# The sums among the MLP's weight factors, made in the mixers' last stage and kept in DRAM

## The chip, the cores and the metric

The kernel runs on one core of a Trainium2 chip. The metric is the time of one execution on the device in microseconds (us); the median of three runs is given, and one further execution was profiled.

## The reference, cut to what matters

```python
h = concatenate([meta, x])                       # 16 + 2048 rows of 1024, one layer
z, xbc, dt, u, gates = split(rmsnorm(h) @ w_in)
y_a = ssd_branch(z, xbc, dt, ...)                # gated SSD mixer
y_b = s5_branch(u, ...)                          # S5 mixer, ends in y @ w_glu
g_a, g_b = split(sigmoid(gates))
h = h + (g_a * y_a + g_b * y_b) @ w_out
hn = rmsnorm(h)
h = h + square(relu(hn @ w_ff_in)) @ w_ff_out    # 1024 -> 4096 -> 1024
out = rmsnorm(h)[16:]                            # float32
```

The change touches only how the factors of `w_ff_in` and `w_ff_out` are prepared.

## The kernel before

Every float32 matrix is split into a rounded high part (type float32r, by a copy on ScalarE) and a low part (a subtraction on VectorE or GpSimd), and each product is three matmuls: high by high, high by low, low by high (`mm3`, lines 244 to 246).

**Mixers.** The 2048 rows go through in four blocks `b` of 512. A block has the input products (weights `wu` by `xnh`, `xnl`) with the SSD and S5 work between them, then its last products: GLU (`y5h`, `y5l` by 8 weight units) and OUT (`mixh`, `mixl` by 8 units). Four PSUM banks of the pool `psd` hold a group's four results; `evac_glu` (VectorE on `gth`) and `evac_out` (VectorE adds `xr`, which SP's queue has loaded, and SP stores the sum to `h2d`) empty them before the next group can fill them. In block 0 a unit is loaded raw (`wst`), split, used and stored (`wsd`), all on SP's queue; in later blocks GpSimd's queue loads the finished `wsd`. Three unit buffers stand for this (`NWU`).

**MLP.** It runs over three batches of rows: 768, 768 and 512 (`FB`). Each batch makes 8 passes (`di`) over the hidden width, and each pass 28 products by Strassen-Winograd's scheme: 7 for each half of `w_ff_in`'s block (`ff_in`) and 7 for each half of `w_ff_out`'s (`ff_out`). Such a group of 7 needs 7 weight factors from four quarters of a pair of weight units: three are quarters themselves, and four are sums or differences (s1 to s4, t1 to t4). Only batch 0 makes the factors (`Weights.make`): SP loads a group's two units into two of four `raw` buffers, GpSimd makes the four sums in five `sum` buffers, and `weight` splits each factor into one of three `wc` buffers (ScalarE the high part, line 1344; VectorE or GpSimd the low part, line 1345, by the list `ENG`: 15 and 13 of 28), uses it and stores it to `wcd` (line 1346). Batches 1 and 2 load the finished factors from `wcd` by GpSimd's queue (`read`, line 1355). Factors are traced one product ahead (`AHEAD`).

A pass of batches 0 to 2 begins with ScalarE's first copy `u<-pd` at line 1457 (two copies in a pass, one for each half). Each engine and each queue executes in the order that the program's scheduler wrote; an instruction that waits holds back what stands behind it.

The part of `weight` that the ring of three buffers hangs on:

```python
t = wcs[0].tile([P, 2, n, 512 // n], F32R, name="wc", tag="wc", bufs=wcs[1])   # 3 buffers
S.copy(t[:, 0], w)
(V if eng == "v" else G).tensor_tensor(t[:, 1], w, t[:, 0].bitcast(F32), op=ALU.subtract)
nc.sync.dma_start(wcd[i], t.rearrange("p a k n -> p (a k n)").bitcast(F32))
```

Of the kernel before, what the change touches and what calls it, by code (L numbers as in the profile page):

```python
# [9 lines left out]
F32 = mybir.dt.float32  # L10
F32R = mybir.dt.float32r
AF = mybir.ActivationFunctionType
ALU = mybir.AluOpType
# [3 lines left out]
P = 128  # L17
# [19 lines left out]
NWC = 5  # L37
NWU = 3
NJK = 1
AHEAD = 1  # L40
NRAW = 4
FPACE = 2
# [85 lines left out]
def _body(ctx, tc, d, out):  # L128
# [3 lines left out]
    def pool(name, bufs=1, stack=ctx, **kw):  # L132
        if "space" not in kw:
            kw["reuse_waits"] = "tile"
        return stack.enter_context(tc.tile_pool(name=name, bufs=bufs, **kw))
# [56 lines left out]
    tabd = dr.tile([P, NQ, 2, KA + 1], F32, name="tabd")  # L192
    h2d = dr.tile([SEQ, D], F32, name="h2d")
    xtd = dr.tile([7, P, 4, FB[1][1] // 2], F32, name="xtd")
    wcd = dr.tile([8 * 28, P, D], F32, name="wcd")
    csd = dr.tile([NB, NC4 * NH, P], F32, name="csd")
    ud = dr.tile([NM + SEQ, 512], F32, name="ud")
# [692 lines left out]
        return t  # L890


    xp = pool("xn", stack=xp_st)

    def load_x(pl, r0, L, src):
# [101 lines left out]
    def ff_raw(pl, nm):  # L997
        return pl.tile([P, D], F32, name=nm, tag="raw", bufs=NRAW)
# [90 lines left out]
    for b in range(NB):  # L1089
# [166 lines left out]
            xn = make_xn(gp, b + 1, xp)  # L1256
        mh = gp.tile([P, 8, TB], F32R, name="mixh")
        ml = gp.tile([P, 8, TB], F32R, name="mixl")
        for q in range(4):
            n = q // 2  # L1260

            def evac_glu(c, p):
                th = gp.tile([P, 256], F32, name="gth", tag="gth", bufs=2)
                S.activation(th, p[:, 256:512], AF.Tanh, scale=0.5)
                V.scalar_tensor_tensor(th, th, 1.0, p[:, 0:256], op0=ALU.add, op1=ALU.mult)
                o = (q % 2) * 256
                V.scalar_tensor_tensor(th, sgbs[n][:, c, o:o + 256], 1.0, th, op0=ALU.add, op1=ALU.mult)
                ma = mixA[:, c, q * 256:(q + 1) * 256]
                G.tensor_tensor(ma, ma, th, op=ALU.add)
            rhs_group([(b, U_GLU + q * 2 + i) for i in range(2)], y5h, y5l, evac_glu)  # L1270
            if q % 2 == 0:
                continue
            for c in range(NC4):
                p = bank("mxp")
                for f in range(4):
                    T.transpose(p[:, f * P:(f + 1) * P], mixA[:, c, n * 512 + f * P:n * 512 + (f + 1) * P], ident)
                pv = p.rearrange("p (f l) -> p f l", f=4)
                a = slice(c * P, (c + 1) * P)
                oh, ol = mh[:, n * 4:n * 4 + 4, a], ml[:, n * 4:n * 4 + 4, a]
                S.activation(oh, pv, AF.Copy, scale=0.25)  # L1280
                V.scalar_tensor_tensor(ol, pv, 0.25, oh.bitcast(F32), op0=ALU.mult, op1=ALU.subtract)
        if b == NB - 1:
            y5_st.close()
            mp_st.close()
            xp_st.close()
            cm_st.close()
            fw = pool("mlpw")
            hp = pool("mlpx", stack=hp_st)
            hn = x_factors(hp, FB[0][1] // 2)
            rows = ff_norm(split_into(hn), lambda nm: ff_raw(fw, nm),  # L1290
                           lambda nm: ff_sum(fw, nm).rearrange("p (f l) -> p f l", f=4), bank, NE[0],
                           FB[0][0], FB[0][1] // 2, 1)
            for _ in rows:
                pass
        for n in range(2):
            def evac_out(c, p, n=n, b=b):
# [5 lines left out]
                jk = gp.tile([P, 512], F32, name="jk", tag="jk", bufs=2)  # L1302
                i = b * NC4 + c
                S.activation(jk, xr, AF.Square, accum_out=ssh[:, n, i:i + 1])
            rhs_group([(b, U_OUT + n * 4 + i) for i in range(4)], mh, ml, evac_out)
        if b < NB - 1:
            V.tensor_tensor(ssh[:, 0, b * NC4:(b + 1) * NC4], ssh[:, 0, b * NC4:(b + 1) * NC4],
                            ssh[:, 1, b * NC4:(b + 1) * NC4], op=ALU.add)
            row_scale(ssh[:, 0, b * NC4:(b + 1) * NC4], rsh[:, b * NC4:(b + 1) * NC4], NC4)
        g_st.close()  # L1310
        if b < NB - 1:
            y5_st.close()
# [13 lines left out]
    class Weights:  # L1326
# [14 lines left out]
        def weight(self, w, eng, n, i):  # L1341

            t = wcs[0].tile([P, 2, n, 512 // n], F32R, name="wc", tag="wc", bufs=wcs[1])
            S.copy(t[:, 0], w)
            (V if eng == "v" else G).tensor_tensor(t[:, 1], w, t[:, 0].bitcast(F32), op=ALU.subtract)  # L1345
            nc.sync.dma_start(wcd[i], t.rearrange("p a k n -> p (a k n)").bitcast(F32))
            return t

        def read(self):
# [6 lines left out]
                    yield t.rearrange("p (a k n) -> p a k n", a=2, k=4 if j < 14 else 2)  # L1356

        def make(self):
            for di in range(ND):
                for half in range(2):  # L1360
                    c = 2 * di + half
                    wa, wb = ff_raw(fw, "w1a"), ff_raw(fw, "w1b")
                    nc.sync.dma_start(wa, d["w"][U_FFI + 2 * c])
                    nc.sync.dma_start(wb, d["w"][U_FFI + 2 * c + 1])
                    a11, a12, a21, a22 = [x.rearrange("p (a k n) -> p a k n", a=2, k=4)[:, i]
                                          for x in (wa, wb) for i in range(2)]
                    s2, s3, s1, s4 = [ff_sum(fw, nm).rearrange("p (k n) -> p k n", k=4)
                                      for nm in ("s2", "s3", "s1", "s4")]
                    G.tensor_tensor(s1, a21, a22, op=ALU.add)
                    G.tensor_tensor(s2, s1, a11, op=ALU.subtract)  # L1370
                    G.tensor_tensor(s3, a11, a21, op=ALU.subtract)
                    G.tensor_tensor(s4, a12, s2, op=ALU.subtract)
                    for j, (w, e) in enumerate(zip((a11, s2, s3, a12, s1, a22, s4), ENG[half])):
                        yield self.weight(w, e, 4, di * 28 + half * 7 + j)
                for n in range(2):
                    b1, b2 = ff_raw(fw, "w2a"), ff_raw(fw, "w2b")
                    nc.sync.dma_start(b1, d["w"][U_FFO + 4 * di + n])
                    nc.sync.dma_start(b2, d["w"][U_FFO + 4 * di + 2 + n])
                    b11, b12, b21, b22 = [x.rearrange("p (k a n) -> p k a n", k=2, a=2)[:, :, i, :]
                                          for x in (b1, b2) for i in range(2)]  # L1380
                    t3, t1, t2, t4 = [ff_sum(fw, nm).rearrange("p (k n) -> p k n", k=2)
                                      for nm in ("t3", "t1", "t2", "t4")]
                    G.tensor_tensor(t3, b22, b12, op=ALU.subtract)
                    G.tensor_tensor(t1, b12, b11, op=ALU.subtract)
                    G.tensor_tensor(t2, b22, t1, op=ALU.subtract)
                    G.tensor_tensor(t4, b21, t2, op=ALU.subtract)
                    for j, (w, e) in enumerate(zip((b11, t3, b21, t4, t1, t2, b22), ENG[2 + n])):
                        yield self.weight(w, e, 2, di * 28 + 14 + n * 7 + j)

        def take(self):  # L1390
            ahead = AHEAD if wcs[0] is fw and self.n == 0 else NRAW + wcs[1] - 2
# [373 lines left out]
```

## Time and profile before

| | us |
|---|---|
| median of 3 runs (lowest to highest) | 3295.41 (3295.22 to 3297.82) |
| the profiled execution's own time | 3295.92 |
| its span, first to last instruction | 3294.2 |
| TensorE busy in the span | 3079.3 (93%) |
| VectorE, ScalarE, GpSimd busy | 2082.6, 1224.1, 1423.9 |

The span is what the profile's views cut into stretches; the execution's own time is 1.7 us longer. Busy shares are averages over stages with different limits, so the views below are read stage by stage. Matmuls are pipelined and their ends are modelled.

### The profile page before, as it was taken

To read this page: it belongs to the slowest core of one execution; us is meant where nothing else is said; L and a number is where in the kernel's file an instruction comes from. 1 tells how busy PE (TensorE), PEld (TensorE's weight loads), DVE (VectorE), ACT (ScalarE), POOL (GpSimd) and SP (SyncE) were. 2 spreads that over 40 slices of the span, in tenths; PEclk is the share of its full clock that TensorE was granted. 3 is DMA by queue.
4 is the path that set the end of the run, shared out by engine and by line. 5 is a ranking of instruction groups with operands and counts; after the bars stand their busy time and mean duration, and the time that the engine had idled before them with its cause. 6 is when DMAs were issued, how large, how long until landed. Compare 5 with 4: busy or idle time off the path is not lost. (4 is left out here: it accounts for less than half of the span.)

```text
span 3294.2 us, 49794 instructions
## 1 busy us (share of the span) xinstructions
PE 3079.3 (93%) x18353; PEld 2749.2 (83%) x18353; DVE 2082.6 (63%) x4153; ACT 1224.1 (37%) x2428; POOL 1423.9 (43%) x1736
## 2 busy tenths in 40 slices
PE   7898999999999999998999899998879999989998
PEld 6687888877887778877888798888879999989998
DVE  8969997427742576426855566676775555575555
ACT  6254454434431443334433333343442121142222
POOL 4356666524421344213433565656642222243443
PEclk9999999999999999999999899999989999999999
DMA  6486676775556554666756777777788888889998
GB/s 219 146 244 191 198 201 219 271 241 164 168 200 215 185 169 159 209 210 203 233 175 217 271 272 261 264 270 256 271 290 275 247 246 245 249 286 374 358 359 277
DMA packets 297875, 782.90 MB, mean 238 GB/s; under 512 B 90688, under 2 KB 132800, under 8 KB 268448
## 3 DMA queue, kind: packets, MB, share of 16 engines
q0 software_dynamic: 88832, 411.21, 37.5%
q1 hardware_dynamic: 206192, 367.29, 34.1%
q8 instruction: 146, 2.39, 0.3%
q10 hardware_dynamic: 2608, 1.22, 0.1%
q14 instruction: 97, 0.79, 0.1%
HBM read 563.66 MB, written 218.05 MB: 237 GB/s over the span
## 5 line engine op out<-in xcount | busy, mean ns | idle before, releaser
L1504 DVE TENSOR_TENSOR acc<-acc,p 128x512 f32<-128x512 f32 x330 | 225.8, 684 | 172.7 <-PE p L246 169.9
L244 PE MATMUL pd<-hnh,wc 128*128 128x384 f32 (+1 forms) x896 | 293.9, 329 | 29.1 <-DMA wc<-wcd 20.6
L244 PE MATMUL pd<-wu,xnh 128*128 128x512 f32 x768 | 311.1, 406 | 2.3 <-ACT cacc L749 1.6
L245 PE MATMUL pd<-wu,xnh 128*128 128x512 f32 x768 | 310.6, 404 | 0.0
L246 PE MATMUL pd<-wu,xnl 128*128 128x512 f32 x768 | 309.2, 403 | 0.0
L246 PE MATMUL pd<-hnh,wc 128*128 128x384 f32 (+1 forms) x896 | 291.9, 329 | 13.6 <-DVE wc L1345 12.2
L245 PE MATMUL pd<-hnl,wc 128*128 128x384 f32 (+1 forms) x896 | 292.8, 327 | 0.0
L228 POOL DMA_DIRECT2D wu<-wsd x168 | 96.5, 574 | 369.5 <-PE pd L246 305.4
L1355 POOL DMA_DIRECT2D wr<-wcd x227 | 122.4, 540 | 275.2 <-PE pd L246 137.1
L244 PE MATMUL pd<-xnh,wu 128*128 128x512 f32 (+1 forms) x640 | 232.2, 363 | 8.4 <-DMA wu<-wsd 8.4
L246 PE MATMUL pd<-xnh,wu 128*128 128x512 f32 (+1 forms) x640 | 229.6, 359 | 0.0
L245 PE MATMUL pd<-xnl,wu 128*128 128x512 f32 (+1 forms) x640 | 229.5, 359 | 0.0
L1355 POOL DMA_DIRECT2D wc<-wcd x221 | 118.9, 538 | 252.7 <-PE pd L246 134.4
L244 PEld LDWEIGHTS pd<-hnh,wc 128*128 128x128 f32 x896 | 174.3, 195 | 34.0 <-ACT hnh L993 12.9
L246 PEld LDWEIGHTS pd<-hnh,wc 128*128 128x128 f32 x896 | 174.0, 194 | 19.1 <-DVE wc L1345 15.7
L752 DVE SCALAR_TENSOR_TENSOR cacc<-craw,conv,cacc 128x512 f32<-128x512 f32 (+1 forms) x192 | 173.7, 906 | 23.1 <-ACT cacc L749 14.8
L218 POOL TENSOR_TENSOR wu<-wst,wu 128x1024 fp32r<-128x1024 f32 x56 | 138.3, 2471 | 100.0 <-ACT wu L217 98.6
L244 PEld LDWEIGHTS pd<-wu,xnh 128*128 128x128 f32 x768 | 147.0, 191 | 34.8 <-ACT cacc L749 2.4
L245 PEld LDWEIGHTS pd<-hnl,wc 128*128 128x128 f32 x896 | 174.7, 195 | 0.0
L245 PEld LDWEIGHTS pd<-wu,xnh 128*128 128x128 f32 x768 | 147.2, 192 | 31.7 <-issue 0.2
L246 PEld LDWEIGHTS pd<-wu,xnl 128*128 128x128 f32 x768 | 146.9, 191 | 31.8
L244 PEld LDWEIGHTS pd<-xnh,wu 128*128 128x128 f32 x640 | 125.1, 196 | 25.3 <-ACT cacc L749 3.6
(1016 smaller groups left out, 9910.3 us busy)
## 6 DMA issues: line engine op xcount, KB each, us to landing
wu<-wsd POOLq DMA_DIRECT2D x168, 1024.0 KB, 5.2
wr<-wcd POOLq DMA_DIRECT2D x227, 512.0 KB, 5.0
wcd<-wc SPq DMA_DIRECT2D x224, 512.0 KB, 3.5
wc<-wcd POOLq DMA_DIRECT2D x221, 512.0 KB, 5.3
wsd<-wu SPq DMA_DIRECT2D x56, 1024.0 KB, 5.3
wst<-in_w SPq DMA_DIRECT2D x60, 512.0 KB, 5.7
csb<-csd SPq DMA_DIRECT2D x16, 1024.0 KB, 12.0
xt<-in_x SPq DMA_DIRECT2D x28, 512.0 KB, 4.7
```

What stands on the lines that cost most here:

```text
L218: eng.tensor_tensor(t[:, 1], raw, t[:, 0].bitcast(F32), op=ALU.subtract)
L228: nc.gpsimd.dma_start(t, wsd[u - U_XBC])
L244: T.matmul(ps, lh, rh, start=first, stop=False, skip_group_check=open_)
L245: T.matmul(ps, lh, rl, start=False, stop=False, skip_group_check=open_)
L246: return T.matmul(ps, ll, rh, start=False, stop=last, skip_group_check=open_).ins
L752: V.scalar_tensor_tensor(acc[:, :n], raw[:, k:k + n], conv[:, mt, k:k + 1], acc[:, :n], op0=ALU.mult, op1=ALU.add)
L1355: nc.gpsimd.dma_start(t, wcd[di * 28 + j])
L1504: V.tensor_tensor(o, o, pv, op=ALU.add)
```

## The change

In each mixer block a generator `ff_early` runs beside the GLU and OUT products (in block 3 beside GLU alone): for 9, 9, 9 and 5 of the 32 groups (`EARLY`) SP loads the group's two raw units (two buffers `er`, one group at a time), VectorE makes its four sums (four buffers `es`), and SP stores each to a new DRAM tensor `smd` (32 x 4 tiles of 128x512 float32, 256 KB each). `rhs_group` calls `early_step` after each unit, which advances the generator in step with the units. Each block drains its generator at its end.

`Weights.make` in MLP batch 0 no longer makes sums. SP loads them from `smd` into the five `sum` buffers, five ahead. The raw units are loaded one group earlier (behind the first factor of the group before), and only the quarters that are factors themselves: the second unit's second half for `w_ff_in`'s groups, the first unit's first column half (1 KB runs) for `w_ff_out`'s. The split, the ring of three `wc` buffers, the stores to `wcd` and the products are as before.

```diff
+EARLY = (9, 9, 9, 5)
+SUMS = {4: (1, 2, 4, 6), 2: (1, 3, 4, 5)}
...
+    smd = dr.tile([32 * 4, P, 512], F32, name="smd")
...
+    def ff_load(g, wa, wb):
+        di, j = divmod(g, 4)
+        ua, ub = (U_FFI + 4 * di + 2 * j, U_FFI + 4 * di + 2 * j + 1) if j < 2 else \
+            (U_FFO + 4 * di + j - 2, U_FFO + 4 * di + j)
+        nc.sync.dma_start(wa, d["w"][ua])
+        nc.sync.dma_start(wb, d["w"][ub])
+    def ff_sums(g, v, room, eng):
+        a11, a12, a21, a22 = v
+        def tt(nm, x, y, op):
+            o = room(nm)
+            eng.tensor_tensor(o, x, y, op=op)
+            return o
+        if g % 4 < 2:
+            s1 = tt("s1", a21, a22, ALU.add)
+            yield 4, s1
+            s2 = tt("s2", s1, a11, ALU.subtract)
+            yield 1, s2
+            yield 2, tt("s3", a11, a21, ALU.subtract)
+            yield 6, tt("s4", a12, s2, ALU.subtract)
+        else:
+            yield 1, tt("t3", a22, a12, ALU.subtract)
+            t1 = tt("t1", a12, a11, ALU.subtract)
+            yield 4, t1
+            t2 = tt("t2", a22, t1, ALU.subtract)
+            yield 5, t2
+            yield 3, tt("t4", a21, t2, ALU.subtract)
+    def ff_split(t, w, eng, i):
+        S.copy(t[:, 0], w)
+        eng.tensor_tensor(t[:, 1], w, t[:, 0].bitcast(F32), op=ALU.subtract)
+        nc.sync.dma_start(wcd[i], t.rearrange("p a k n -> p (a k n)").bitcast(F32))
+    def ff_early(pl, groups):
+        def load(g):
+            wa, wb = [pl.tile([P, D], F32, name=nm, tag="er", bufs=2) for nm in ("era", "erb")]
+            ff_load(g, wa, wb)
+            return wa, wb
+        raw = load(groups[0])
+        for n, g in enumerate(groups):
+            v, m = ff_pieces(g, *raw)
+            def room(nm):
+                return pl.tile([P, 512], F32, name=nm, tag="es", bufs=4).rearrange("p (k n) -> p k n", k=m)
+            for j, w in ff_sums(g, v, room, V):
+                nc.sync.dma_start(smd[g * 4 + SUMS[m].index(j)], w.rearrange("p k n -> p (k n)"))
+                if j == (6 if m == 4 else 3) and n + 1 < len(groups):
+                    raw = load(groups[n + 1])
+                yield
...
+        e_st = ExitStack()
+        g0 = sum(EARLY[:b])
+        early = ff_early(pool("early%d" % b, stack=e_st, side="right"), range(g0, g0 + EARLY[b]))
+        slots = 8 if b == NB - 1 else 16
+        early_n = [0, 0]
+
+        def early_step(mm):
+            early_n[0] += 1
+            want = -(-early_n[0] * EARLY[b] * 4 // slots)
+            with tc.issue_after(mm):
+                while early_n[1] < want:
+                    early_n[1] += 1
+                    next(early, None)
...
-            rhs_group([(b, U_GLU + q * 2 + i) for i in range(2)], y5h, y5l, evac_glu)
+            rhs_group([(b, U_GLU + q * 2 + i) for i in range(2)], y5h, y5l, evac_glu, step=early_step)
...
         if b == NB - 1:
+            for _ in early:
+                pass
+            e_st.close()
...
-            rhs_group([(b, U_OUT + n * 4 + i) for i in range(4)], mh, ml, evac_out)
+            rhs_group([(b, U_OUT + n * 4 + i) for i in range(4)], mh, ml, evac_out, step=early_step if b < NB - 1 else None)
...
-                    G.tensor_tensor(s1, a21, a22, op=ALU.add)
...
+            raws, sums = [], []
+            more = ((g, k) for g in range(32) for k in range(4))
+            def load_raws(g):
+                di, j = divmod(g, 4)
+                a, b = [ff_raw(fw, nm) for nm in ("wa", "wb")]
+                if j < 2:
+                    u = U_FFI + 4 * di + 2 * j
+                    nc.sync.dma_start(a, d["w"][u])
+                    nc.sync.dma_start(b[:, 512:], d["w"][u + 1][:, 512:])
+                else:
+                    u = U_FFO + 4 * di + j - 2
+                    nc.sync.dma_start(a.rearrange("p (k a n) -> p k a n", k=2, a=2)[:, :, 0, :],
+                                      d["w"][u].rearrange("p (k a n) -> p k a n", k=2, a=2)[:, :, 0, :])
+                    nc.sync.dma_start(b, d["w"][u + 2])
+                raws.append((a, b))
+            def load_sum():
+                g, k = next(more, (None, 0))
+                if g is not None:
+                    t = ff_sum(fw, "sm")
+                    nc.sync.dma_start(t, smd[g * 4 + k])
+                    sums.append(t)
+            load_raws(0)
+            for _ in range(NSUM):
+                load_sum()
+            for g in range(32):
+                (a11, a12, a21, a22), m = ff_pieces(g, *raws.pop(0))
+                ws = {0: a11, 3: a12, 5: a22} if m == 4 else {0: a11, 2: a21, 6: a22}
+                for j in range(7):
+                    w = ws[j] if j in ws else sums.pop(0).rearrange("p (k n) -> p k n", k=m)
+                    t = self.weight(w, ENG[g % 4][j], m, g * 7 + j)
+                    if j not in ws:
+                        load_sum()
+                    if j == 0 and g < 31:
+                        load_raws(g + 1)
+                    yield t
```

## Rows read from the trace of the kernel before

**Rows 1.** The page's head: the span, and TensorE's busy time, share and instructions.
```profile
span 3294.2 us, 49794 instructions
...
PE 3079.3 (93%) x18353; PEld 2749.2 (83%) x18353; DVE 2082.6 (63%) x4153; ACT 1224.1 (37%) x2428; POOL 1423.9 (43%) x1736
```

**Rows 2.** Windows: GLU with OUT by block, block 3 apart, MLP batches 0 and 1.
```profile
core 0: us, PE busy (x) PEld busy (x) DVE busy (x) ACT busy (x) POOL busy (x), PEclk, DMA share, GB/s
583.20:684.50 101.30, 100.62 (x472) 80.54 (x471) 40.66 (x64) 38.45 (x66) 46.85 (x32) 1.00 0.75 269
964.90:1064.50 99.60, 99.60 (x468) 80.10 (x467) 34.65 (x63) 23.99 (x50) 20.64 (x32) 1.00 0.58 200
...
1731.70:1778.50 46.80, 46.80 (x212) 37.52 (x211) 17.14 (x34) 11.57 (x25) 14.72 (x22) 1.00 0.58 198
1779.40:1847.70 68.30, 59.87 (x288) 49.66 (x286) 40.30 (x55) 28.36 (x57) 30.45 (x27) 0.95 0.73 249
1847.70:2440.20 592.50, 518.69 (x3361) 499.39 (x3359) 408.09 (x563) 234.62 (x430) 356.31 (x263) 0.95 0.75 271
2440.20:2934.30 494.10, 486.39 (x3392) 482.50 (x3392) 289.44 (x484) 118.32 (x237) 145.70 (x242) 0.99 0.82 251
```

**Rows 3.** Timeline of ScalarE: pass 1 and pass 7 of batch 0 begin, then of batch 1.
```profile
1914.89 0.48 ACT L1457 COPY u<-pd 128x384 f32<-128x384 f32 x1 [2.86 <-PE pd L246]
...
2348.61 0.48 ACT L1457 COPY u<-pd 128x384 f32<-128x384 f32 x1 [2.86 <-PE pd L246]
...
2509.11 0.48 ACT L1457 COPY u<-pd 128x384 f32<-128x384 f32 x1 [14.02 <-PE pd L246]
...
2867.36 0.48 ACT L1457 COPY u<-pd 128x384 f32<-128x384 f32 x1 [23.80 <-PE pd L246]
```

**Rows 4.** Waits in batch 0: us in total, times, longest us.
```profile
ACT wc L1344 <- DMA wcd<-wc: 115.1, 81, 4.1
POOL t L1383 <- DMA w2b<-in_w: 62.9, 12, 6.8
```

**Rows 5.** Groups of GpSimd in batch 0: busy us, mean ns, idle before.
```profile
L1345 POOL TENSOR_TENSOR wc<-t,wc 128x512 fp32r<-128x512 f32 x32 | 46.2, 1442 | 10.0 <-ACT wc L1344 10.0
...
L1384 POOL TENSOR_TENSOR t<-w2a 128x512 f32<-128x512 f32 x16 | 25.2, 1576 | 0.6 <-DVE wc L1345 0.6
...
L1369 POOL TENSOR_TENSOR s<-w1b 128x512 f32<-128x512 f32 x14 | 18.7, 1338 | 41.3 <-DMA w1b<-in_w 32.2 <-DMA wcd<-wc 5.1 <-DVE acc L1504 4.0
```

**Rows 6.** Groups of VectorE: three of batch 0, then one of batch 1.
```profile
L1422 DVE TENSOR_TENSOR fs4l<-fa,fs4h 128x384 fp32r<-128x384 f32 x16 | 19.8, 1242 | 0.0
...
L1345 DVE TENSOR_TENSOR wc<-w2b,wc 128x512 fp32r<-128x512 f32 x16 | 11.6, 723 | 1.4 <-ACT wc L1344 1.4
...
L1504 DVE TENSOR_TENSOR acc<-acc,p 128x512 f32<-128x512 f32 x110 | 75.1, 683 | 47.1 <-PE p L246 46.3
...
L1422 DVE TENSOR_TENSOR fs4l<-fa,fs4h 128x384 fp32r<-128x384 f32 x16 | 9.8, 614 | 0.1
```

**Rows 7.** DMA issues of the span: count, KB each, median us to landing.
```profile
wcd<-wc SPq DMA_DIRECT2D x224, 512.0 KB, 3.5
...
w1a<-in_w SPq DMA_DIRECT2D x16, 512.0 KB, 4.7
...
w2b<-in_w SPq DMA_DIRECT2D x16, 512.0 KB, 6.0
```

**Rows 8.** ScalarE's group of the factors' high parts, around batch 0.
```profile
L1344 ACT CAST wc<-t 128x512 fp32r<-128x512 f32 x64 | 39.6, 619 | 73.0 <-DMA wcd<-wc 28.4 <-PE px L246 13.2 <-DVE acc L1504 13.0
```

**Rows 9.** Windows with the highest DMA rates: in batch 2, and at batch 0's end.
```profile
2960.00:3040.00 80.00, 74.11 (x585) 73.30 (x586) 43.14 (x88) 15.73 (x40) 30.57 (x54) 0.96 1.08 376
...
2400.00:2420.00 20.00, 18.62 (x145) 18.42 (x144) 11.15 (x16) 9.28 (x13) 10.66 (x9) 1.00 1.03 393
```

**Rows 10.** Waits in the mixers, 560 to 1778 us.
```profile
DVE xr L1300 <- DMA xr<-in_x: 55.7, 10, 10.9
```

**Rows 11.** All loads of raw weight units.
```profile
DMA to landing us min/median/max: 4.2/5.8/9.1
```

More of the change, by code (lines that the diff above doesn't have):

```diff
@@ L890, in decays, with ff_pieces @@
         return t
+    def ff_pieces(g, wa, wb):
+        if g % 4 < 2:
+            v = [x.rearrange("p (a k n) -> p a k n", a=2, k=4)[:, i] for x in (wa, wb) for i in range(2)]
+            return v, 4
+        v = [x.rearrange("p (k a n) -> p k a n", k=2, a=2)[:, :, i, :] for x in (wa, wb) for i in range(2)]
+        return v, 2
+    def ff_load(g, wa, wb):
[10 more added lines that the diff above has]
+            return o
+        if g % 4 < 2:
+            s1 = tt("s1", a21, a22, ALU.add)
[30 more added lines that the diff above has]
+                yield
     xp = pool("xn", stack=xp_st)
@@ L1309, in _body @@
             row_scale(ssh[:, 0, b * NC4:(b + 1) * NC4], rsh[:, b * NC4:(b + 1) * NC4], NC4)
+        for _ in early:
+            pass
+        e_st.close()
         g_st.close()
@@ L1343, in weight @@
             t = wcs[0].tile([P, 2, n, 512 // n], F32R, name="wc", tag="wc", bufs=wcs[1])
-            S.copy(t[:, 0], w)
-            (V if eng == "v" else G).tensor_tensor(t[:, 1], w, t[:, 0].bitcast(F32), op=ALU.subtract)
-            nc.sync.dma_start(wcd[i], t.rearrange("p a k n -> p (a k n)").bitcast(F32))
+            ff_split(t, w, V if eng == "v" else G, i)
             return t
@@ L1358, in make @@
         def make(self):
[L1359 to L1368, printed above, removed]
-                    G.tensor_tensor(s1, a21, a22, op=ALU.add)
[L1370 to L1388, printed above, removed]
```

## The prediction

> **What bounds the kernel now.** I read the head of the page first: TensorE is busy for 93% of the span [rows 1], so a change pays only where TensorE waits. The windows by stage show where that is [rows 2]. In the mixers' last products it never waits: 99.6 of 99.6 us in block 1, 100.6 of 101.3 in block 0, 46.8 of 46.8 in block 3's GLU. In MLP batch 0 it is busy for 518.7 of 592.5 us at a granted clock of 0.95; batch 1, with the same products on factors that are loaded ready, takes 494.1 us at 0.99. The timeline gives the pace without the batches' ends [rows 3]: passes 1 to 6 of batch 0 take (2348.6 - 1914.9) / 6 = 72.3 us each, those of batch 1 (2867.4 - 2509.1) / 6 = 59.7. Making the factors therefore costs at most 592.5 - 494.1 = 98 us, and this is the most that the change can give in batch 0.
>
> What holds batch 0 up is shared. The list of waits names ScalarE's cast into a `wc` buffer, which stands 115.1 us in all until an earlier factor's store to `wcd` has landed, and GpSimd, which waits 62.9 us for raw units before t3 alone [rows 4]: a group's loads are issued only when the group before is used up. GpSimd is busy for 356 us [rows 2]; its eight groups of sums (first and last in [rows 5]) add up to 172 us of that. And VectorE's two-input work on SBUF stretches while GpSimd works: the `fs4l` subtraction takes 1242 ns in batch 0 and 614 ns in batch 1; its work with an operand in PSUM keeps 683 ns [rows 6]. So late accumulations, late factors and late raws all reach TensorE.
>
> **The change part by part.**
>
> *Sums off GpSimd in batch 0.* 172 us of 356 go, and with them roughly half of VectorE's stretching. No sum waits for a raw unit in front of the products any more: raws are issued six factors ahead and sums five sums ahead, some 13 us at batch 1's pace against landings of 4.7 to 6.0 us [rows 7]. All that remains to make a factor is cast, subtraction, store.
>
> *The ring of three `wc` buffers* stays. A buffer is held for the cast, 0.62 us [rows 8], the subtraction, 0.72 us on VectorE [rows 6] or 1.44 on GpSimd [rows 5], and the landing of its store, 3.5 us in the median [rows 7]: 4.8 or 5.6 us, over three buffers 1.6 or 1.9 us for a product, where batch 1's pace is 59.7 / 28 = 2.13. So the ring is no bound as long as landings stay short; it becomes one at 4.3 us (GpSimd's 13 factors) and 5.1 us (VectorE's 15). At 4.8 us a pass would take 15 x 2.13 + 13 x 2.29 = 61.7 us; at 6.0 us, the landing of today's `w2b`, 15 x 2.45 + 13 x 2.69 = 71.7, and nothing would be gained. These are the ends.
>
> *DMA of batch 0.* It moves 271 GB/s x 592.5 us = 160.6 MB now [rows 2]. Added are 128 sums of 256 KB (33.6 MB); 256 KB of raws a group are saved (8.4 MB): 185.7 MB, 23.2 a pass. What the engines carry I bound by rows: 361 GB/s if the share of 0.75 at 271 is scaled to 1; 376 in the fastest 80 us, 393 in the fastest 20 us [rows 9]. At 361 a pass takes 64.3 us. This is slower than the ring at 4.8 us, and I take it: passes 1 to 6 gain 8.0 us each, pass 0 (1847.7 to 1914.9, 67.2 us) gains 2.9, the last, 91.6 us with the change of batch in it, 8.0. Together **-59 us**, within 0 and -98.
>
> *Sums in the mixers: VectorE.* 36 sums at about 0.69 us (the 128x512 rows in [rows 6]) are 25 us in blocks 0 to 2, 14 in block 3. VectorE is busy for 41, 35, 35 and 17 us there [rows 2], so there is room, and I cost the work itself at nothing: TensorE's own 99.6 us hide it. In what order the queues take it is another matter, below.
>
> *Sums in the mixers: DMA.* A group loads 1 MB and stores 1 MB, 2.1 million bytes in all: 18.9 MB in blocks 0 to 2, 10.5 in block 3, all on SP's queue, beside `xr`, `h2d` and, in block 0, `wst` and `wsd`. With what the windows show [rows 2], block 0 has 27.2 + 18.9 = 46.1 MB, blocks 1 and 2 have 19.9 + 18.9 = 38.8, block 3's GLU 9.3 + 10.5 = 19.8. At 376 GB/s that is 122.7, 103.2 and 52.6 us, over today's 101.3, 99.6 and 46.8 by 21.4, 3.6 (twice) and 5.8: 34 us. At 361 it is 50 us, at 393 20 us. This is the only place where TensorE has no slack at all, so the excess appears in full unless it can trail: a last group (5.6 us) may run beneath the next block's products in blocks 0 to 2, which takes 12.8 off. I take **+22 us**; ends 0 (all trails) and 50.
>
> On this the Trainium skill ("DMA: Bandwidth & Descriptors", section Bandwidth) speaks against the change: for transfers between HBM and SBUF it lets the HBM's share for a core, about 358 GB/s, bind. By that the mixers' sum would be +54 us (my estimate from its figure). The rows show 376 over 80 us [rows 9], so I give it little weight, as a rival below.
>
> *GpSimd's queue in the mixers* carries no new DMA; the loads of `wu` in blocks 1 to 3 share the DMA engines but not the queue. In block 0 `wst` and `wsd` stand in SP's queue between the stores of sums, each of which waits for VectorE, and the 6.3 us that a unit takes must hold all of it.
>
> *Start of batch 0.* Its raws and five sums are issued where today's first raws are; TensorE's 8 us of idle in the window before [rows 2] I leave as they are.
>
> **Sum.** 3295.9 (the profiled execution; 0.5 above the median of the runs, so the same for this purpose) - 59 + 22 = **3259 us**.
>
> **The rivals.**
>
> *VectorE's order (slower).* VectorE executes in order, and of each group the first sum waits for raws, of which only one group is in flight. Landing, four sums and the next issue make a chain of about 5.8 + 2.8 + 1 = 10 us [rows 11], nine times in 100 us: it only just fits. When the DMA is at its limit, landings go towards 9.1 us [rows 11] and VectorE stands 3.3 us longer in front of `gth` and `xr`, whose banks TensorE needs. If 24 of the 32 groups cost TensorE that, it is +79 us: 3259 + 79 = 3338; it decides from 37 / 32 = 1.2 us lost a group. Against it: VectorE waits for `xr` for up to 10.9 us today [rows 10] while block 1's products run without a gap [rows 2]. In block 0 and 3 I find it quite possible.
>
> *The ring stays the bound.* With stores landing after 5.6 us, a pass takes 15 x 2.31 + 13 x 2.55 = 67.8 us: 8 x 4.5 less, 34 more in the mixers, 3294. The change then moves work and does nothing. For it: 350 GB/s on one queue; against it: landings of 3.5 us at 271 GB/s.
>
> *All of it hidden.* If batch 0 comes down to batch 1's 59.7 us and the mixers cost 20: 3295.9 - 98 + 20 = 3218. For it: batch 2 moves 376 GB/s with TensorE busy for 74 of 80 us [rows 9]; against it: those factors are only read, not made.
>
> *The DMA limit is at 361 GB/s.* The engines carry no more than today's shares scaled to 1, and nothing trails: mixers +50, batch 0 -59, which makes 3287. Against it: the 376 of [rows 9]. The figure of the Trainium skill named above, "DMA: Bandwidth & Descriptors", section Bandwidth, would come out three microseconds above this.
>
> **How the numbers follow.** Chances: forecast 0.49 (own range 3235 to 3282), all hidden 0.12, the DMA limit 0.09, the ring 0.12, VectorE's order 0.18. A measurement of this kernel tells 0.2%, 6.6 us, from no change. Faster are the forecast, all hidden, and most of the DMA limit's and some of the ring's: 0.70. Same: the rest of these two, 0.09. Slower: VectorE's order and a bad ring, 0.21. The range goes from the full gain to just above no change, 3214 to 3304; it leaves out most of VectorE's order.
>
> **What would show it.** Right: passes of batch 0 near 64 us, no wait of GpSimd for raws, `fs4l` well under 1.2 us, DMA near 350 GB/s there; in block 0's last products 110 to 117 us at over 370 GB/s, about 100 in blocks 1 and 2. Wrong: the cast's wait for `wcd` stays near 115 us and landings rise past 5 us; or TensorE shows gaps in GLU and OUT that end on `gth`, `xr` or `wu`, with the granted clock at 0.5 behind them, and VectorE's sums wait for `era` and `erb`.

## The result, and the profile after

The changed kernel takes 3329.58 us in the median of four runs (3326.38 to 3332.25), the kernel before 3296.61 beside it: a ratio of 1.0097, 95% interval 1.0081 to 1.0113. It is slower by 33 us; 3259 was forecast, with a range up to 3304. One execution of `e3_no_sums` below took 10335.57 us beside 3315.97 to 3325.00 and is left out of its median. The page's head of the profiled execution (3326.38 us) shows nothing of why: TensorE is busy for as long as before, within 1 us [rows 1].

```profile
span 3324.7 us, 50383 instructions
...
PE 3080.2 (93%) x18353; PEld 2743.8 (83%) x18353; DVE 2104.8 (63%) x4281; ACT 1222.2 (37%) x2428; POOL 1238.9 (37%) x1608
```

The windows by stage do, against [rows 2]. The first three are GLU and OUT of blocks 0, 1 and 2 (from the first GLU product to the next block's first input product), the fourth block 3's GLU, the fifth its OUT with what follows up to batch 0, the last two MLP batches 0 and 1.

```profile
core 0: us, PE busy (x) PEld busy (x) DVE busy (x) ACT busy (x) POOL busy (x), PEclk, DMA share, GB/s
583.40:709.40 126.00, 108.02 (x474) 84.25 (x472) 57.05 (x96) 38.41 (x65) 50.60 (x34) 0.95 0.95 364
989.10:1106.10 117.00, 104.96 (x471) 82.48 (x469) 55.35 (x96) 24.39 (x51) 21.63 (x32) 0.97 0.88 315
1384.00:1505.70 121.70, 105.74 (x472) 82.96 (x471) 54.44 (x96) 24.22 (x51) 20.71 (x32) 0.96 0.85 301
1794.50:1847.20 52.70, 48.84 (x222) 38.73 (x221) 26.62 (x51) 12.55 (x26) 15.08 (x22) 1.00 0.92 322
1847.20:1918.20 71.00, 61.53 (x290) 51.14 (x289) 39.46 (x56) 28.49 (x57) 19.42 (x19) 0.93 0.76 256
1918.20:2460.70 542.50, 496.94 (x3357) 483.44 (x3355) 353.41 (x562) 233.43 (x430) 184.05 (x141) 0.98 0.93 336
2460.70:2964.20 503.50, 485.88 (x3392) 482.83 (x3392) 289.08 (x486) 117.53 (x236) 144.84 (x244) 0.98 0.82 251
```

Cut in the same way in both traces, the balance is this (GLU + OUT runs from the first GLU product to the next block's first input product, in block 3 to the first `u` of batch 0):

| us | block 0 | block 1 | block 2 | block 3 | batch 0 | batch 1 | all else |
|---|---|---|---|---|---|---|---|
| before | 101.6 | 99.9 | 99.9 | 116.0 | 592.5 | 494.1 | 1790.2 |
| after | 126.0 | 117.1 | 121.6 | 123.7 | 542.5 | 503.6 | 1790.2 |
| difference | +24.4 | +17.2 | +21.7 | +7.7 | -50.0 | +9.5 | 0.0 |

So the mixers lose 71 us and batch 0 gives 50. In block 1, TensorE stands still for 12.0 us in all and its busy time rises by 5.4 us, for the same products, at a clock of 0.97: together its 17.4 us in the windows. The list of TensorE's waits in block 1's GLU and OUT names only short things:

```profile
PE pd L247 <- DMA wu<-wsd: 7.8, 3, 3.0
PE pd L247 <- DVE xr L1383: 2.8, 1, 2.8
```

What stands behind them is in the queues, VectorE's first and then SP's (us in total, times, longest):

```profile
DVE s L918 <- DMA erb<-in_w: 14.3, 3, 10.3
DVE gth L1345 <- ACT gth L1344: 9.1, 6, 4.7
DVE t L918 <- DMA erb<-in_w: 8.1, 3, 4.5
...
SPq L954 <- DVE t L918: 30.8, 9, 8.5
SPq L1384 <- DVE xr L1383: 18.4, 6, 10.5
SPq L954 <- DVE gth L1347: 14.1, 6, 11.2
SPq L954 <- DVE s L918: 11.0, 8, 5.2
```

L918 is a sum, L954 its store to `smd`, L1383 the addition of `xr` that empties an OUT bank. One of the gaps, in order of time, from the timeline of SP, VectorE and TensorE:

```profile
1077.70 0.53 SPq L910 DMA_DIRECT2D erb<-in_w  x1
1078.33 1.63 SPq L1382 DMA_DIRECT2D xr<-in_x  x2
...
1086.35 0.69 DVE L918 TENSOR_TENSOR s<-erb 128x512 f32<-128x512 f32 x1 [10.34 <-DMA erb<-in_w]
1087.05 0.69 DVE L1383 TENSOR_TENSOR xr<-xr,pd 128x512 f32<-128x512 f32 x1
...
1087.80 0.50 PE L247 MATMUL pd<-wu,mixh 128*128 128x512 f32 x1 [2.77 <-DVE xr L1383]
```

`erb`, issued at 1077.70, holds VectorE for 10.34 us; the addition behind it in the queue, which needs nothing of the sum, comes only then, and TensorE waits 2.77 us for its bank. The waits that end on `wu` follow in part from such stops, as GpSimd issues a `wu` load only when TensorE is done with a buffer:

```profile
1095.44 0.54 POOL L231 DMA_DIRECT2D wu<-wsd  x1 [21.00 <-PE pd L249]
...
1100.58 0.50 PE L247 MATMUL pd<-wu,mixh 128*128 128x512 f32 x1 [2.71 <-DMA wu<-wsd]
```

That load landed after 5.1 us, as loads do in the kernel before, but GpSimd's queue had stood for 21.0 us before it was issued (12.2 at the same place before). In block 2's GLU the chain is longer. A sum whose raw was issued at 1405.66 holds VectorE for 7.10 us; the second step of `gth` stands behind it, GpSimd's addition to `mixA` waits for that, and TensorE's transposition for the addition:

```profile
1419.59 0.69 DVE L918 TENSOR_TENSOR s<-erb 128x512 f32<-128x512 f32 x1 [7.10 <-DMA erb<-in_w]
1420.20 0.42 DVE L1347 SCALAR_TENSOR_TENSOR gth<-sgb,gth 128x256 f32<-128x256 f32 x1
...
1421.85 0.69 PE L1356 MATMUL mxp<-ident,mixA 128*128 128x128 f32 x2 [5.45 <-POOL mixA L1349]
```

In block 1 loads also take longer from issue to landing (median us, last column): `wu` 7.5 where the kernel before has 5.1.

```profile
wu<-wsd POOLq DMA_DIRECT2D x16, 1024.0 KB, 7.5
...
erb<-in_w SPq DMA_DIRECT2D x7, 512.0 KB, 8.6
```

Batch 0 is faster. Passes 1 and 7 begin where ScalarE's timeline shows these copies [rows 3]; passes 1 to 6 take (2380.03 - 1982.72) / 6 = 66.2 us, 72.3 before.

```profile
1982.72 0.48 ACT L1550 COPY u<-pd 128x384 f32<-128x384 f32 x1 [2.24 <-PE pd L249]
...
2380.03 0.48 ACT L1550 COPY u<-pd 128x384 f32<-128x384 f32 x1 [2.60 <-PE pd L249]
```

GpSimd falls from 356 to 184 us there [rows 2], its sums with their waits for raws [rows 4] being gone, and `fs4l` from 1242 to 844 ns [rows 6]. But the wait that the forecast called a sign of failure has grown, from 115.1 [rows 4] to 160.2 us:

```profile
ACT wc L937 <- DMA wcd<-wc: 160.2, 119, 3.7
...
L1515 DVE TENSOR_TENSOR fs4l<-fa,fs4h 128x384 fp32r<-128x384 f32 x16 | 13.5, 844 | 0.0
```

### The profile page after: what moved, and what is told of

The parts are those of the page before. It is cut to its first block, busy times and chain, and to the rows that moved or that the text cites. A ratio compares the mean times of both kernels' runs of the same rounds, so it can differ in the third digit from the quotient of the medians.

```text
span 3324.7 us, 50383 instructions
## 1 busy us (share of the span) xinstructions
PE 3080.2 (93%) x18353; PEld 2743.8 (83%) x18353; DVE 2104.8 (63%) x4281; ACT 1222.2 (37%) x2428; POOL 1238.9 (37%) x1608
## 5 line engine op out<-in xcount | busy, mean ns | idle before, releaser
L247 PE MATMUL pd<-hnh,wc 128*128 128x384 f32 (+1 forms) x896 | 288.3, 323 | 19.3 <-DMA wc<-wcd 11.9
L249 PE MATMUL pd<-hnh,wc 128*128 128x384 f32 (+1 forms) x896 | 289.9, 324 | 1.4 <-DVE wc L938 0.9
L247 PEld LDWEIGHTS pd<-hnh,wc 128*128 128x128 f32 x896 | 171.3, 191 | 20.6 <-issue 12.2
L249 PEld LDWEIGHTS pd<-wu,xnl 128*128 128x128 f32 x768 | 146.2, 190 | 32.2
L247 PEld LDWEIGHTS pd<-xnh,wu 128*128 128x128 f32 x640 | 126.5, 198 | 29.8 <-issue 10.2
```

The source lines that it names most:

```text
L247: T.matmul(ps, lh, rh, start=first, stop=False, skip_group_check=open_)
L249: return T.matmul(ps, ll, rh, start=False, stop=last, skip_group_check=open_).ins
```

## The experiments

In the tables a column is a stage as above, read from one profiled execution of each kernel. Losses are against the kernel before. GLU runs from its first product to OUT's first, OUT from there to the next block's first input product: for blocks 1 and 2 GLU takes 51.3 + 51.3 and OUT 48.6 + 48.6 us before, 58.7 + 64.3 and 58.4 + 57.3 after. Block 3's stage moves by up to 3 us where nothing is added to it (-0.9 in `e1_mlp_half`, -3.0 in `e11_spread`).

**The two halves.** `e1_mlp_half` is the kernel after without the mixers' part, and its batch 0 loads pieces of the weights in the place of sums (its edits are shown); `e2_mixer_half` is the kernel after with `Weights.make` of the kernel before.

```diff
-EARLY = (9, 9, 9, 5)
+EARLY = (0, 0, 0, 0)
...
-                    nc.sync.dma_start(t, smd[g * 4 + k])
+                    nc.sync.dma_start(t, d["w"][U_FFI + (g * 4 + k) % 64][:, :512])
```

> The MLP half alone: nothing is added to the mixers, and batch 0 loads its 128 sums from pieces of the weights (256 KB each, the values are not the sums). If batch 0's gain and the mixers' loss are independent, the time is that of before less the 50 us that batch 0 gained, about 3246 us, and batch 1's first pass stays at 69 us. A rival, that batch 0's gain is partly the later start (work moved ahead of it), would give 3260 us or more.

> The mixers' half alone: the sums are made and stored in the mixers, but batch 0 makes its own sums on GpSimd as before. If the mixers carry the whole loss, the time is that of before plus about 70 us, 3367 us, with block 0's last products at 126 us and blocks 1 and 2 at 117 to 122. If part of the loss belongs to batch 0's start or to batch 1's first pass, it is under 3350 us.

| | median us | ratio (95%) | blocks 0 to 3 | batch 0 | batch 1 |
|---|---|---|---|---|---|
| MLP half | 3254.16 | 0.9870 (0.9855 to 0.9885) | +0.0 +0.0 +1.3 -0.9 | 546.3 | 500.7 |
| mixers' half | 3367.42 | 1.0207 (1.0185 to 1.0229) | +21.9 +19.3 +21.5 +12.8 | 590.1 | 493.7 |

The halves add up: (3254.16 - 3296.88) + (3367.42 - 3296.88) = -42.7 + 70.5 = +28 us, the whole +33. The 5 us between them are within the intervals, so neither half is seen to disturb the other: batch 0's gain does not pay for the mixers. The MLP half gained 43 us where 50 were expected, and batch 1's first pass takes 75.5 us in it, not 69.

**Without VectorE's sums.** `e3_no_sums` stores the raws themselves, four stores a group.

```diff
-            for j, w in ff_sums(g, v, room, V):
-                nc.sync.dma_start(smd[g * 4 + SUMS[m].index(j)], ...)
+            for i in range(4):
+                nc.sync.dma_start(smd[g * 4 + i], raw[i // 2][:, (i % 2) * 512:(i % 2) * 512 + 512])
```

> The whole change without VectorE's sums: the four stores of a group take quarters of the raw units themselves (the same bytes, the values are not the sums). If the loss in the mixers comes from sums that wait for raws in VectorE's queue, it falls from 70 us to 25 or less and the time is 3270 to 3285 us. If it comes from the DMA traffic (late wu and xr), it stays at 50 to 70 us and the time is 3310 to 3330 us.

It took 3316.42 us, 1.0067 (1.0046 to 1.0087). The blocks together lose 64.6 us, which its expectation put down to the traffic. But blocks 1 and 2 lose 28.5 us, where they lost 38.9: GLU 5.1 instead of 20.4, OUT 23.4 instead of 18.5. So VectorE's queue is GLU's trouble, not OUT's. The stores still stand in SP's queue in front of `xr`, now waiting for raws.

**More groups in flight.** `e5_two_groups` loads a group's raws before the sums of the group ahead of it.

```diff
-            wa, wb = [pl.tile([P, D], F32, name=nm, tag="er", bufs=2) for nm in ("era", "erb")]
+            wa, wb = [pl.tile([P, D], F32, name=nm, tag="er", bufs=4) for nm in ("era", "erb")]
...
+            if n + 1 < len(groups):
+                raws.append(load(groups[n + 1]))
```

> The whole change with raws for two groups in flight (four buffers instead of two), so that a sum's raws are issued a group earlier. If VectorE's wait for raws is the cause, blocks 1 and 2 fall from 117 to 122 us to about 105 and the time to 3285 us. If the traffic is the cause, blocks stay within 3 us of the change and the time is 3320 to 3330 us, since the same bytes only come earlier.

3317.18 us, 1.0055 (1.0037 to 1.0073), between the two expectations: blocks 0 to 3 lose 25.0, 16.0, 11.0 and 3.1, but block 3's input products take 300.8 us instead of 287.7. OUT of blocks 1 and 2 loses 6.0, GLU 21.0, although VectorE waits for no raw in these GLU stages any more. They run at 351 and 372 GB/s, at a share of 0.97 and 0.99: the traffic has moved forward into them. One group more in flight is no cure.

**Raws earlier, in the kernel before.** `e4_prefetch` changes nothing but the place of the raws' loads in batch 0's program: behind the first factor of the group before, as the change does it. The sums stay with GpSimd.

```diff
+                for j, (w, e) in enumerate(zip(fs, ENG[g % 4])):
+                    t = self.weight(w, e, m, g * 7 + j)
+                    if j == 0 and g < 31:
+                        load_raws(g + 1)
+                    yield t
```

> The kernel before with one thing of the change: batch 0's raw units are loaded one group earlier; GpSimd still makes the sums and the mixers are untouched. If late raws were what held batch 0 up, most of the 43 us of the MLP half comes back without any traffic in the mixers: 3255 to 3270 us. If it was GpSimd's 172 us of sums (and VectorE's stretching beside them), the time stays near that of before: 3285 to 3300 us.

3293.92 us, 0.9996 (0.9987 to 1.0005), batch 0 592.6 us. That is no answer on late raws, for the loads did not move. In passes 1 to 6 SP issues the eight raws of a pass at the same times after its start, within 0.4 us in the mean (the first after 6.7 us, 6.4 before), and GpSimd still waits for them, 104.7 us in these two lines where it was 95.1 (62.9 for t3 [rows 4], 32.2 for s1 [rows 5]):

```profile
POOL t L1388 <- DMA wb<-in_w: 75.0, 13, 11.3
...
POOL s L1378 <- DMA wb<-in_w: 29.7, 11, 4.2
```

What raws that come earlier would be worth to the kernel before stays open.

**A queue of their own for `xr` and `yt`.** `e6_own_queue` loads both by ScalarE's queue and gives `xr` four buffers instead of two; the two edits were not tried apart.

```diff
-            nc.sync.dma_start(yt, yd[r0:r0 + P, :])
+            nc.scalar.dma_start(yt, yd[r0:r0 + P, :])
...
-                xr = gp.tile([P, 512], F32, name="xr", tag="xr", bufs=2)
-                nc.sync.dma_start(xr, ...)
+                xr = gp.tile([P, 512], F32, name="xr", tag="xr", bufs=4)
+                nc.scalar.dma_start(xr, ...)
```

> The whole change with the loads of xr (four buffers instead of two) and yt issued by ScalarE's queue, so that they no longer stand behind the sums' stores in SP's. If SP's order is what delays the evacuation of OUT's banks, and with it the release of the wu buffers, OUT falls from 57 to 58 us to about 50 in blocks 0 to 2 and the time to 3300 us or less. If the traffic alone is the cause, wu still lands after 7 us and more, and the time is 3320 to 3335 us.

3304.31 us, 1.0029 (1.0018 to 1.0041). OUT of blocks 1 and 2 takes 48.8 and 50.4 us (in block 2 its own products end after 48.6, and the next product waits 1.8 us for an `xr`); GLU stays bad, 69.8 and 60.5. The timeline of VectorE and TensorE shows GLU's mechanism in block 1, the same as above: a sum whose raw was issued at 1006.76 holds VectorE for 8.44 us, with the subtraction for `xnl` behind it, on which TensorE's next transposition of `mixA` waits.

```profile
1020.19 0.69 DVE L918 TENSOR_TENSOR s<-erb 128x512 f32<-128x512 f32 x1 [8.44 <-DMA erb<-in_w]
1020.80 1.28 DVE L281 TENSOR_TENSOR xnl<-ntp,xnh 128x512 fp32r<-128x512 f32 x2
...
1021.63 0.66 PE L1356 MATMUL mxp<-ident,mixA 128*128 128x128 f32 x2 [8.59 <-DVE xnl L281]
```

**Sums, raws and stores apart.** `e7_sums_alone` has neither raws nor stores, `e8_no_stores` raws and sums, `e9_no_raws` sums and stores. Where there are no raws, VectorE fills the two buffers once a block; where there are no stores, batch 0 loads quarters of raw units in the sums' place.

```diff
-            ff_load(g, wa, wb)
+            V.memset(wa, 1.0)
+            V.memset(wb, 1.0)
...
-                nc.sync.dma_start(smd[g * 4 + SUMS[m].index(j)], w.rearrange("p k n -> p (k n)"))
```

> The change with VectorE's 128 sums alone in the mixers: taken from two resident tiles, no raws loaded and no sums stored there (batch 0 loads pieces of the weights instead of sums). If VectorE's work itself is hidden, the time is that of the MLP half alone, 3254 us, within 5. If it costs TensorE, it is 3270 us or more.

> The change with raws loaded and sums made in the mixers, but not stored: half of the added traffic, and nothing in SP's queue that waits for VectorE but the raws' own buffers (batch 0 loads pieces of the weights). If the waits of sums for raws are the cause, the mixers still lose 45 us or more and the time is 3300 us or more. If it is traffic or the stores' place in SP's queue, they lose half or less: 3275 to 3290 us.

> The change with sums and stores in the mixers but no raws loaded: the sums come from two resident tiles (wrong values, right sizes), so nothing waits for a landing, and the added traffic is the 1 MB of stores a group. If the bytes of the stores cost TensorE, the mixers still lose 40 us or more (of 71) and the time is 3290 us or more. If the cost is the chain from landing to sum to store to the next load in SP's queue, the loss falls to 20 us or less and the time is 3275 us or less.

| in the mixers | median us | ratio (95%) | block 0 | blocks 1 + 2 | block 3 |
|---|---|---|---|---|---|
| sums alone | 3262.10 | 0.9894 (0.9878 to 0.9910) | +10.2 | +0.5 | -2.8 |
| raws, sums | 3271.78 | 0.9931 (0.9905 to 0.9956) | +15.3 | +8.7 | +1.4 |
| sums, stores | 3287.95 | 0.9976 (0.9965 to 0.9987) | +18.1 | +8.8 | +7.3 |
| raws, stores | 3316.42 | 1.0067 (1.0046 to 1.0087) | +21.4 | +28.5 | +14.7 |
| all (after) | 3329.58 | 1.0097 (1.0081 to 1.0113) | +24.4 | +38.9 | +7.7 |

In blocks 1 and 2 the sums cost nothing by themselves and either half of the traffic 4.4 us a block; both halves together cost 14 to 19. So waits alone are not the price either: in block 1 of raws and sums VectorE waits 18.8 us for raws, and the block loses 4.1. The sums alone and the sums with stores came out between their expectations. Block 1's windows, of sums alone and of raws and sums:

```profile
974.80:1075.00 100.20, 100.11 (x469) 80.41 (x468) 42.01 (x77) 24.11 (x50) 20.44 (x32) 1.00 0.57 199
```

```profile
981.90:1085.90 104.00, 100.81 (x472) 80.44 (x471) 54.44 (x96) 24.24 (x51) 20.69 (x32) 1.00 0.75 265
```

In block 0 the sums alone cost 10.2 us. Its timeline with sums alone, VectorE then TensorE, shows them in a row in front of `y5l`. As nothing there holds them back, neither raws nor stores, they have run in rows since before the stage began, so this price need not be the change's:

```profile
586.05 0.68 DVE L918 TENSOR_TENSOR s<-erb 128x512 f32<-128x512 f32 x1
586.77 0.69 DVE L918 TENSOR_TENSOR s<-s,era 128x512 f32<-128x512 f32 x1
587.38 2.83 DVE L918 TENSOR_TENSOR s<-era,erb 128x512 f32<-128x512 f32 x1
590.14 0.68 DVE L1316 TENSOR_TENSOR y5l<-y5p,y5h 128x512 fp32r<-128x512 f32 x1
...
590.87 0.50 PE L249 MATMUL pd<-wu,y5l 128*128 128x512 f32 x1 [3.83 <-DVE y5l L1316]
```

One of them takes 2.83 us there instead of 0.69; why is open.

**Both cures.** `e10_both` joins `e5_two_groups` with the queue of their own for `xr` (three buffers) and `yt`.

> The whole change with both reliefs: raws for two groups in flight, and the loads of xr (three buffers) and yt on ScalarE's queue. If order in the queues is the cause, GLU and OUT of blocks 1 and 2 fall to 105 us or less together, and the time to 3280 to 3295 us; block 0 stays at 120 us or more, because its bytes alone need that. If traffic is the cause everywhere, blocks 1 and 2 stay at 111 us or more and the time is 3300 us or more.

3317.50 us, 1.0054 (1.0037 to 1.0071). Not the sum of two gains: OUT of blocks 1 and 2 loses 5.4 us, GLU 18.2, and block 3 17.9. By its expectation (blocks 1 and 2 at 111 us or more, 3300 us or more) this is the traffic's outcome, and the windows of the two GLU stages bear it out, at a share of 0.99:

```profile
997.90:1056.90 59.00, 53.93 (x260) 43.91 (x257) 41.44 (x75) 16.80 (x33) 15.68 (x21) 0.97 0.99 375
1389.70:1451.60 61.90, 54.75 (x260) 43.91 (x258) 44.37 (x78) 16.61 (x33) 14.83 (x21) 0.97 0.99 376
```

Where the queues let loads and stores run ahead, the bytes crowd into GLU; OUT then runs at 277 and 258 GB/s.

**Spread over a longer stage.** `e11_spread` runs the generator beside the input products of blocks 1 to 3 instead.

```diff
-EARLY = (9, 9, 9, 5)
+EARLY = (0, 11, 11, 10)
...
-            rhs_group(..., y5h, y5l, evac_glu, step=early_step)
+            rhs_group(..., y5h, y5l, evac_glu)
```

> The whole change with the sums made beside the input products of blocks 1 to 3 (11, 11 and 10 groups, 32 steps each) instead of beside GLU and OUT; block 0 makes none. The added traffic is then some 23 MB over 280 us instead of 19 MB over 100. If traffic in a short stretch is the cause, GLU and OUT return to 100 us and the input stages lose under 8 us each: 3260 to 3280 us. If VectorE's order is the cause, the input stages, where VectorE is busier, lose 15 us or more each and the time is 3300 us or more.

3353.09 us, 1.0173 (1.0158 to 1.0188), and not a test of what it was for. VectorE and SP do not wait for TensorE's steps: they run ahead as far as their buffers allow, and block 1's first sums and stores already ran beside block 0's OUT, from 649 us on. So blocks 0 to 2 lost 14.5, 10.8 and 12.5 us there, and the input products of blocks 1 to 3 another 13.9, 31.3 and 20.6.

**Batch 0 without DRAM.** `e12_vector` is `e4_prefetch` with all sums on VectorE, in batch 0 itself; `e13_shared` has two of four there.

```diff
-                    G.tensor_tensor(s1, a21, a22, op=ALU.add)
+                    V.tensor_tensor(s1, a21, a22, op=ALU.add)
```

> The kernel before with the raw units of a group loaded one group earlier (as in the run before this one that moved the time by nothing) and all 128 sums of batch 0 made by VectorE instead of GpSimd; nothing is done in the mixers and nothing more goes through DRAM. Theory (batch 0 was slow because GpSimd made the sums, not because they were made there): GpSimd falls from 356 to some 184 us in batch 0, VectorE rises from 353 to 353 + 128 x 0.69 = 441 us of some 550, batch 0 takes 540 to 560 us against 592.5, blocks 0 to 3 keep their times to 1 us, in all 3296 - 45 = 3251 us (3240 to 3265). Rival (VectorE's time is worth as much as GpSimd's, 88 us more of it in front of the accumulations hold TensorE): batch 0 takes 580 us or more, 3283 to 3310 us.

> As the run beside it, but two of a group's four sums (s3, s4; t3, t4) on VectorE and two on GpSimd. Theory that GpSimd's sums hold batch 0, each as much as the other: half the gain, batch 0 near 568 us, 3296 - 24 = 3272 us (3262 to 3282). Rival (GpSimd had only to come below a point, and VectorE is the one that has no time to give): as good as or better than the run beside it, under 3258 us. Second rival (the two engines wait for each other through s1 to s4): no gain, 3290 us or more.

3259.04 us, 0.9894 (0.9878 to 0.9911), and 3263.47 us, 0.9907 (0.9890 to 0.9924). Both beat the kernel before and the kernel after, for `e12_vector` by 35 and some 70 us, with nothing in the mixers. Batch 0's windows, of all sums on VectorE and then of two of four:

```profile
1842.30:2400.80 558.50, 509.05 (x3361) 490.29 (x3360) 452.04 (x684) 233.63 (x430) 196.54 (x142) 0.96 0.79 288
```

```profile
1844.80:2411.30 566.50, 507.09 (x3362) 483.38 (x3361) 441.87 (x624) 234.03 (x429) 280.74 (x202) 0.98 0.78 283
```

The theory holds, and so does the one of `e13_shared`: VectorE has the time (452 of 558 us), and passes 1 to 6 take 67.3 us each by ScalarE's copies, about as after the change, at 288 GB/s instead of 336. Half of the sums give more than half of the gain, 26 of 34 us.

**The traffic alone.** `e14_traffic_only` joins `e3_no_sums` and `e6_own_queue`: all bytes, no sums, `xr` and `yt` on their own queue.

> The kernel after without VectorE's sums (the raws themselves are stored in their place, so the factors are not the reference's) and with xr and yt loaded on ScalarE's queue, xr in four buffers: the mixers' whole traffic stays, about 2.1 million bytes a group at 300 to 330 GB/s in the stretch, but nothing waits in VectorE's queue for raws and no xr stands behind a store. Over the kernel before, blocks 1 and 2 lost 38.9 us after the change; without the sums GLU lost 6 and OUT 23, with the loads on their own queue but the sums kept GLU lost 28 and OUT 0. Theory (two queues in order: GLU pays for VectorE's, OUT for SP's; the traffic itself is nearly free): blocks 1 and 2 lose 4 to 10 us in all, blocks 0 to 3 together 20 to 30 instead of 71, the kernel takes 3265 to 3285 us. Rival (the traffic makes the loads of wu late whatever the order): blocks 1 and 2 lose 20 us or more, GLU and OUT alike, and the kernel takes 3300 us or more.

3292.54 us, 0.9990 (0.9975 to 1.0005). Blocks 0 to 3 lose 22.2, 4.6, 6.5 and -0.5: 33 us instead of 71. All three figures lie a little above the theory's (11.1 us in blocks 1 and 2 for 4 to 10, 33 for 20 to 30, and the total), because block 0 kept its loss and block 3's input products took 302.2 us, 14.5 longer, which was not traced. In blocks 1 and 2 GLU loses 11.6 and OUT nothing (48.3 and 48.4), at the highest mean rate over both blocks of any of these kernels (the lines are blocks 0, 1 and 2):

```profile
582.90:706.70 123.80, 108.78 (x475) 85.05 (x474) 39.34 (x66) 39.85 (x69) 48.79 (x33) 0.93 0.98 375
981.60:1086.10 104.50, 100.55 (x471) 80.54 (x470) 36.18 (x65) 24.30 (x52) 20.58 (x32) 1.00 0.98 346
1365.70:1472.00 106.30, 102.19 (x470) 81.31 (x468) 35.55 (x64) 24.11 (x51) 20.41 (x32) 0.98 0.94 329
```

`wu` lands after 8.0 us there in the median, later than the 7.5 after the change. So late `wu` loads explain at most these 11 us; 28 of the 39 us in blocks 1 and 2 are what the order of the queues makes of this traffic.

## Why the prediction was wrong

**The mixers: the step that failed.** The forecast cost VectorE's 25 us of sums "at nothing", put the order of the queues aside as "another matter, below", and made the whole charge out of bytes over 376 GB/s: 21.4 in block 0, 3.6 in blocks 1 and 2, 5.8 in block 3, less 12.8 that would trail. Measured: 24.4, 17.2, 21.7 and 7.7. So:

- Block 0 came near its size, 24.4 for 21.4, in part by luck. For the bytes speaks that it runs at 364 GB/s with a share of 0.95, and that `e14_traffic_only` keeps 22.2 there at 375 GB/s and a share of 0.98, next to the 376 that the forecast took. The Trainium skill ("DMA: Bandwidth & Descriptors", section Bandwidth) has about 358 GB/s bind between HBM and SBUF; the traces do not show it as a ceiling, as both means lie above it. Against bytes alone speaks that TensorE's longest waits after the change are 8.8 us for `yt`, whose loads stand in SP's queue too, that the sums alone cost 10.2 us at 245 GB/s, and that `wst` and `wsd` stay in SP's queue in every kernel here. Bytes and order were not separated in this block.
- Blocks 1 and 2 were mis-sized, 38.9 for 7.2, and this is 32 of the 49 us by which the mixers' term failed (71 for 22). The bytes do not set this price: the blocks run at 315 and 301 GB/s, and with the same bytes at 346 and 329 they lose 11.1. The other 28 us go when the sums leave VectorE's queue and `xr` and `yt` leave SP's. In GLU it is VectorE's queue: without its sums the loss falls from 20.4 to 5.1 us, and from 27.7 to 11.6 where `xr` and `yt` have their own queue. In OUT it is SP's, where `xr` stands behind stores that wait for sums or raws: 18.5 us after, 2.0 in `e6_own_queue`, none in `e14_traffic_only`. Sums without traffic cost 0.5 us in these two blocks: the price is not VectorE's work but what it waits for.
- The trailing did not come: 12.8 us more.
- Block 3 came out near, 7.7 for 5.8 (5.0 of it in GLU), but at 322 GB/s, below the 376 that sized it.

**The rival that came nearest**, VectorE's order, gave 3338 and had a chance of 0.18. Its chain was seen, waits of up to 10.34 us for raws in front of `xr`, and the time was near. But its price was 79 us on top of the 22 for bytes, 3.3 us in 24 of the 32 groups by VectorE alone, and the mixers lost 71 in all. In blocks 1 and 2 taking out the sums alone gives 10.4 us, moving `xr` and `yt` alone 9.2, both 27.8: with one queue relieved the other still holds, so the parts cannot simply be added. Its counter-argument, that VectorE already waits for `xr` for 10.9 us [rows 10] without a gap in block 1's products, misled. The 10.9 us end at 694.4 us, beside block 1's input products; in block 1's OUT the longest such wait is 8.5 us, and it comes once. One such wait is covered, several in a stretch whose other loads are late as well are not. That last sentence is argued; `e8_no_stores` speaks for it, where with the waits for raws but half of the traffic, at 265 GB/s, block 1 loses 4.1 us.

**Batch 0** was right in size, -50 for -59, but the reason given is not borne out. Passes of 66.2 us answer to the forecast's 64.3, which came from 361 GB/s as the limit. Passes 1 to 6 run at 334 GB/s with a share of 0.92, and `e12_vector` makes nearly the same passes (67.3) with 288 GB/s in the batch, so the bytes need not have set them. It was the sums on GpSimd: taking them off gives 34 us with the sums made in place by VectorE and 50 with the sums loaded. How much of this is GpSimd's work and how much its waits for raws is open: with VectorE making the sums, the waits for raws in front of them fall from 95 to 26 us, and `e4_prefetch` did not move the loads, although its program places them as the change does, a step that the forecast counted on. The ring of `wc` buffers did not become the bound in the way of the rival "the ring stays", which wanted stores that land after 5.6 us for its 67.8: they land after 4.3 in the median. ScalarE waits longer for them, 160.2 us, and the passes are shorter all the same; that ScalarE now arrives earlier at the same ring is argued, not shown. That sign was chosen badly. What holds a pass at 66 instead of 59.7 us was not isolated.

**Batch 1**, not in the sum, lost 9.5 us, nearly all in its first pass, in which TensorE has one gap of 9.7 us that ends on ScalarE's `fs1h`. It is no fixed price of the change: of the kernels with loaded sums, batch 1 takes 500.7 in `e1_mlp_half` and 495.0 in `e8_no_stores`. Its cause stays open.

**The whole**: 71.0 - 50.0 + 9.5 = 30.5 us, the difference of the two spans. The medians differ by 33.

## What to carry to other kernels

When work is put beside products that never wait, ask of each of its instructions what it waits for and what stands behind it in its queue; bytes over a rate and busy time over a span answer neither. Give the added loads and stores a queue in which nothing that TensorE needs soon stands behind them. Loading a group earlier was no substitute: it took VectorE's waits away and brought GLU's bytes to a share of 0.97 and 0.99. And before work is moved to another stage, through DRAM, try it on another engine where it is: here this alone gave 35 us, and the move cost 71.

## What the runs showed of the hardware

The DMA engines carried more than the forecast's highest window of 393 GB/s [rows 9]: 420 and 412 GB/s over 20 us in block 0 after the change.

```profile
660.00:680.00 20.00, 19.14 (x84) 15.20 (x82) 6.73 (x10) 5.23 (x8) 5.47 (x3) 1.00 1.03 420
580.00:600.00 20.00, 13.75 (x54) 10.58 (x53) 5.69 (x10) 6.04 (x10) 6.14 (x4) 0.84 1.02 412
```

In block 1 of `e14_traffic_only` OUT ran at 362 GB/s and a share of 1.01 while TensorE was busy for every microsecond of it:

```profile
1037.70:1086.10 48.40, 48.40 (x219) 38.55 (x218) 8.96 (x14) 7.95 (x19) 5.84 (x10) 1.00 1.01 362
```

Over a hundred microseconds TensorE kept within 5% of its time at a mean of 346 GB/s with `wu` landing after 8.0 us, yet lost 17% at 315: a mean rate in a window doesn't tell whether its loads are late where it counts.
